# The second product of both MLPs as Strassen's seven products of halves

## The chip, the core and the metric

The kernel runs on one core of a Trainium2 chip. What counts is the time of one execution on the device in microseconds. The core's engines each work through a list of instructions of their own in a fixed order: PE (TensorE) multiplies matrices, PEld is its weight load, DVE (VectorE) and ACT (ScalarE) work element by element, POOL (GpSimd) does some sums, and SP issues the loads from memory. An instruction waits for another engine by a semaphore, and everything behind it in its engine's list waits with it. Sums of matmuls collect in PSUM, everything else lies in SBUF.

## The reference

Two transformer blocks run one after the other on 512 tokens of 1024 features (one batch), in fp32. Each ends with an MLP of 4096 hidden units; their lines are, cut to them:

```python
D_MODEL = 1024
SEQ = 512
D_FF = 4 * D_MODEL
...
        u = rmsnorm_2(x, norm_mlp_g[i]) @ w_up[i]
        x = x + jnp.square(jax.nn.relu(u)) @ w_down[i]
```

The first block's MLP has the same form, with `norm_ffn`, `ffn_w1` and `ffn_w2`. Its block holds a hybrid mixer (spatial gating and a gated delta rule) and a cross attention ahead of the MLP, and a last norm behind it. The second block has an mLSTM and a sliding-window attention ahead of its MLP, and behind it a gate with a small product of `p` (the PLE part).

## The kernel before, in words

All activations lie feature by feature: `x_fm` is x as 8 tiles of 128 features by 512 tokens, and a tile of a product is 128 features by 512 tokens in one PSUM bank. An fp32 product is made of three matmuls (`mm3`, L217 to L222): each operand is split into a high part rounded to the type fp32r and the low rest; high times high (L220), high times low (L221) and low times high (L222) are summed in the bank.

Weights come in pieces of 512 KB, 512 rows by 256 columns, through `wload` (L194 to L205): SP loads the piece into `wr` (2 buffers), ACT casts it to the high part `wh` (L203, 128x1024), DVE subtracts to get `wl` (L204); `wh` and `wl` have 3 buffers each. Two such pieces are a granule: the weights of two output tiles over a depth of 1024, 48 matmuls of 128x512 (`proj_fm` with `wgran`). All of it lies in one tile pool, `wp`, that is open for the whole program, so the loads, casts and subtractions of one stage's first granules stand ready while the stage before still multiplies.

The MLP (`ffn`) goes by quarters of 1024 hidden units. `up(q)` makes 8 hidden tiles in 4 granules: DVE does relu and the token's norm factor from PSUM (L804), ACT squares (L805), and `split_sb` (L261 on ACT, L262 on DVE) writes the high and the low part. `down(q)` is 4 granules of two output tiles each, and DVE adds each finished tile to `x_fm` (`add_res`, L401). H has two sets of buffers (slots 0 to 3 and 4 to 7), so the order is up 0, up 1, down 0, up 2, down 1, up 3, down 2, down 3: every down has another quarter's up ahead of it.

In the last down of an MLP the evacuation also makes the next norm's operands for the tile that has just been finished. Behind the first MLP (`between`) that is the scaled split (L264 on ACT, L265 on DVE) and two squares (L274 on ACT) that are summed into two accumulators (L276, on POOL, for the last tile on DVE); then `fin` sums over features on PE (L284, and a second such sum at L852). Behind the second MLP (`tail`) it is the split and one square.

The order in each engine's list is set by the framework's scheduler when the program is built, from the order in which the kernel writes the instructions and from which buffers come free; there is no order written by hand.

## Time and profile before

| | |
|---|---|
| median of 3 runs | 1758.17 us (1754.64 to 1764.05) |
| the profiled execution | 1758.89 us, its span 1757.1 us |
| mean granted TensorE clock | 0.992 |
| first MLP, roughly | 457 to 815 us of the span |
| second MLP, roughly | 1333 to 1695 us |
| loaded by the hardware queue | 153.64 MB, 27.4% of the DMA engines' time |

The span is the time from the first to the last instruction in the trace. A row of a timeline has the start and the duration in microseconds, engine, line, operation, what is written from what is read, the tile and, in brackets, how long the engine had been idle before it and who ended that. Matmuls overlap: what one costs is the distance from its start to the next one's. A row of a group has the count, the sum and the mean in ns. The windows view has, for each stretch, the busy time and the number of instructions of each engine, then the granted clock, the share of the DMA engines and GB/s.

### The profile page before, as it was taken

The page shows a single profiled execution, that of the slowest core. Times are in us where ns is not written, and L with a number is a line of the kernel's source. Part 1 is how long each engine was busy: PE and PEld are TensorE (multiplying, and loading weights), DVE is VectorE, ACT ScalarE, POOL GpSimd, SP SyncE. Part 2 cuts the span into 40 slices and gives each one's busy share as a digit, 9 for nine tenths or more (in the row PEclk, how much of TensorE's full clock was granted, in tenths as well). Part 3 has the DMA queues.
Part 4 walks back from the last instruction along what each step waited for, and adds up shares of the span by engine and source line. Part 5 has one row for each costly group of instructions (what it writes and reads, how often), then busy time and mean ns, then how long its engine had stood idle before and what let it go on. Part 6 is the DMA issues. An engine that isn't in the chain of part 4 may idle for free.

```text
span 1757.1 us, 22629 instructions
## 1 busy us (share of the span) xinstructions
PE 1719.7 (98%) x8740; PEld 1427.2 (81%) x8740; DVE 1011.4 (58%) x2039; ACT 720.9 (41%) x1254; POOL 148.4 (8%) x126
## 2 busy tenths in 40 slices
PE   7999999999999999999999999999999999999997
PEld 6987788877888888888888887788888888888886
DVE  6898886655543444446755469865555434344446
ACT  5344444444333333334444448654234323232343
POOL 2211321201000000012000000000120000000112
PEclk9999998999999999999999999999999999999999
DMA  5221232312222223223222321223222222323231
GB/s 196 88 72 61 71 97 77 118 51 72 96 97 96 93 89 95 95 86 95 73 73 74 95 73 49 72 73 96 86 97 89 91 95 96 96 96 108 90 102 61
DMA packets 49436, 155.09 MB, mean 88 GB/s; under 512 B 9392, under 2 KB 11696, under 8 KB 49328
## 3 DMA queue, kind: packets, MB, share of 16 engines
q1 hardware_dynamic: 49328, 153.64, 27.4%
q8 instruction: 69, 1.13, 0.3%
q14 instruction: 39, 0.32, 0.1%
HBM read 151.26 MB, written 2.10 MB: 87 GB/s over the span
## 4 chain that ended last, share of the span: by engine, by line
PE 87%; DVE 9%; ACT 2%; issue 2%; DMA 0%; POOL 0%; SPq 0%; DVEq 0%; ACTq 0%
PE psd L221 26%; PE psd L222 26%; PE psd L220 26%; DVE wl L204 1%; PE c L563 1%; ACT wh L203 1%; PE lg L1147 1%; PE po L1174 1%; PE c L512 1%; PE m L1068 1%; DVE S L368 1%; DVE e L319 1%; PE pss L1169 0%; PE m L1076 0%; DVE dA L583 0%
## 5 line engine op out<-in xcount | busy, mean ns | idle before, releaser
L220 PE MATMUL psd<-S,wh 128*128 128x512 f32 (+1 forms) x1968 | 770.5, 392 | 6.3 <-ACT wh L203 6.3
L222 PE MATMUL psd<-S,wl 128*128 128x512 f32 (+1 forms) x1968 | 774.3, 394 | 1.3 <-DVE wl L204 1.3
L221 PE MATMUL psd<-S,wh 128*128 128x512 f32 (+1 forms) x1904 | 748.1, 393 | 2.4 <-DVE S L265 2.3
L204 DVE TENSOR_TENSOR wl<-wr,wh 128x1024 fp32r<-128x1024 f32 (+3 forms) x281 | 349.4, 1243 | 227.0 <-ACT wh L203 225.9
L203 ACT CAST wh<-wr 128x1024 fp32r<-128x1024 f32 (+3 forms) x281 | 292.0, 1039 | 434.3 <-PE psd L221 406.5
L220 PEld LDWEIGHTS psd<-S,wh 128*128 128x128 f32 x1968 | 372.7, 189 | 86.2 <-ACT wh L203 7.2
L222 PEld LDWEIGHTS psd<-S,wl 128*128 128x128 f32 x1968 | 371.5, 189 | 79.8 <-DVE wl L204 2.3
L221 PEld LDWEIGHTS psd<-S,wh 128*128 128x128 f32 x1904 | 358.7, 188 | 80.6 <-DVE S L265 4.2
L276 POOL TENSOR_TENSOR acc<-acc,sq 128x512 f32<-128x512 f32 (+1 forms) x47 | 67.9, 1446 | 916.8 <-ACT sq L274 916.3
L401 DVE TENSOR_TENSOR x_fm<-psd,x_fm 128x512 f32<-128x512 f32 x88 | 60.7, 690 | 137.8 <-PE psd L222 137.7
L221 PE MATMUL psd<-wl,S 128*128 128x256 f32 (+2 forms) x480 | 137.4, 286 | 0.6 <-DVE wl L204 0.6
L222 PE MATMUL psd<-wh,S 128*128 128x256 f32 (+2 forms) x480 | 137.1, 286 | 0.0
L220 PE MATMUL psd<-wh,S 128*128 128x256 f32 (+2 forms) x480 | 136.5, 284 | 0.0
L804 DVE SCALAR_TENSOR_TENSOR e<-psd,bc 128x512 f32<-128x512 f32 x64 | 44.3, 691 | 112.2 <-PE psd L222 109.3
L805 ACT ACTIVATE e<-e 128x512 f32<-128x512 f32 x64 | 40.4, 632 | 135.1 <-DVE e L804 135.1
L221 PEld LDWEIGHTS psd<-wl,S 128*128 128x128 f32 x480 | 91.6, 191 | 1.4 <-DVE wl L204 1.0
L220 PEld LDWEIGHTS psd<-wh,S 128*128 128x128 f32 x480 | 91.8, 191 | 0.4
L222 PEld LDWEIGHTS psd<-wh,S 128*128 128x128 f32 x480 | 91.8, 191 | 0.1
L262 DVE TENSOR_TENSOR S<-e,S 128x512 fp32r<-128x512 f32 (+1 forms) x84 | 56.7, 675 | 49.2 <-ACT S L261 49.2
L261 ACT CAST S<-e 128x512 fp32r<-128x512 f32 (+1 forms) x84 | 50.5, 601 | 42.9 <-POOL e L931 27.1
L264 ACT ACTIVATE S<-x_fm,vec 128x512 fp32r<-128x512 f32 x40 | 28.9, 721 | 55.4 <-DVE x_fm L401 36.9
L319 DVE SCALAR_TENSOR_TENSOR e<-e,vec,e 128x511 f32<-128x511 f32 (+2 forms) x60 | 46.6, 779 | 2.6 <-ACT e L316 2.2
(411 smaller groups left out, 1459.7 us busy)
## 6 DMA issues: line engine op xcount, KB each, us to landing
wr<-in_ffn_w_dram SPq DMA_DIRECT2D x64, 512.0 KB
wr<-in_w_up_dram SPq DMA_DIRECT2D x32, 512.0 KB
wr<-in_w_down_dram SPq DMA_DIRECT2D x32, 512.0 KB
wr<-in_w_in_qk_dram SPq DMA_DIRECT2D x16, 512.0 KB
wr<-in_w_in_v_dram SPq DMA_DIRECT2D x12, 512.0 KB
wr<-in_xa_wk_dram SPq DMA_DIRECT2D x8, 512.0 KB
wr<-in_xa_wv_dram SPq DMA_DIRECT2D x8, 512.0 KB
wr<-in_xa_wq_dram SPq DMA_DIRECT2D x8, 512.0 KB
```

The costliest lines, as they stand in the source:

```text
L203: nc.scalar.copy(hi[:, c], raw[:, c])
L204: nc.vector.tensor_tensor(out=lo[:, c], in0=raw[:, c], in1=hi[:, c].bitcast(F32), op=ALU.subtract)
L220: mm(ps, ah, bh, start=first, stop=False)
L221: mm(ps, ah, bl, start=False, stop=False)
L222: mm(ps, al, bh, start=False, stop=last)
L261: nc.scalar.copy(hi, src)
L262: nc.vector.tensor_tensor(out=lo, in0=src, in1=hi.bitcast(F32), op=ALU.subtract)
L276: eng.tensor_tensor(out=acc, in0=acc, in1=sq, op=ALU.add)
L319: nc.vector.scalar_tensor_tensor(out=c[:, s:], in0=xr[:, :T - s], scalar=w(j), in1=c[:, s:], op0=ALU.mult, op1=ALU.add)
L401: self.nc.vector.tensor_tensor(out=self.x[:, o], in0=ps, in1=self.x[:, o], op=ALU.add)
L804: nc.vector.scalar_tensor_tensor(out=t, in0=ps, scalar=0.0, in1=bc, op0=ALU.max, op1=ALU.mult)
L805: nc.scalar.activation(t, t, AF.Square)
```

## The change

The second product of both MLPs is computed with Strassen's scheme in Winograd's form. For each pair of output tiles the product over 1024 hidden units is taken as a 2x2 block product: two output tiles by the two halves of the hidden units on the one side, the two halves of the hidden units by two halves of the tokens (256 each) on the other. Seven block products take the place of eight. Each is 4 hidden tiles deep, so 4 x 3 matmuls of 128x256, 84 a granule in place of 48 of 128x512.

- The hidden operand: `st_fill` makes four sums and differences of 128x256 on DVE for each pair of hidden tiles, and splits seven blocks (7 x 256 columns in place of 2 x 512) into high and low parts.
- The weights: `st_weights` loads three pieces on SP (512, 512 and 256 KB); a DMA issued by POOL adds the fourth quarter to both halves of the second piece (512 KB, `accum_op`), which gives two of the four weight sums; two DVE additions of 128x512 give the others. Seven blocks are split, in pieces of 1024, 1024, 1024 and 512 columns.
- The products: `st_gemm` puts them into three banks. X takes products 0, 3, 5 and 6, each added to the bank's content; Z takes 2 and 4; Y takes 1. After each product DVE adds or subtracts the bank in one 256-token half of an output tile of x: 7 instructions of 128x256 in place of 2 of 128x512. A later product of the same bank therefore waits for DVE's earlier reading.
- The order: up and down follow each other quarter by quarter, with one set of H. The norm work of the last quarter (`post`) follows the granule.
- The pools: `wp` is closed and opened anew around each MLP, with 5 buffers in place of 3 for `wh` and `wl` there, beside a pool `fp` and a PSUM pool `px`. Slots are renamed to fit, xattn's output pairs and the PLE part's tiles lie elsewhere, and `p` is loaded at the start of `tail`.
- The weights of the second product are laid out by `halves` before the launch.

```diff
+    @contextmanager
+    def weights(self, bufs=3):
+        with self.tc.tile_pool(name=self.uid("wp"), bufs=bufs) as self.wp:
+            yield
...
-        mm(ps, ah, bh, start=first, stop=False)
-        mm(ps, ah, bl, start=False, stop=False)
-        mm(ps, al, bh, start=False, stop=last)
+        mm(ps, ah, bh, start=first, stop=False, skip_group_check=more)
+        mm(ps, ah, bl, start=False, stop=False, skip_group_check=more)
+        mm(ps, al, bh, start=False, stop=last, skip_group_check=more)
...
-        up(0)
-        up(1)
-        down(0, self.add_res)
-        up(2)
-        down(1, self.add_res)
-        up(3)
-        down(2, self.add_res)
-        down(3, evac)
...
+    def st_fill(self, H, k, e1, e2):
+        nc = self.nc
+        TT, STT = nc.vector.tensor_tensor, nc.vector.scalar_tensor_tensor
+        t = H[0]
+        h = (slice(0, 256), slice(256, 512))
+        ms = self.t(self.fp, [P, 4, 256], "ms", bufs=1)
+        TT(out=ms[:, 3], in0=e2[:, h[1]], in1=e1[:, h[1]], op=ALU.subtract)
+        TT(out=ms[:, 1], in0=e1[:, h[0]], in1=e1[:, h[1]], op=ALU.subtract)
+        STT(out=ms[:, 2], in0=ms[:, 3], scalar=-1.0, in1=e1[:, h[0]], op0=ALU.mult, op1=ALU.subtract)
+        STT(out=ms[:, 0], in0=ms[:, 2], scalar=-1.0, in1=e2[:, h[0]], op0=ALU.mult, op1=ALU.subtract)
+        self.split_sb(t[6][:, 0, k], t[6][:, 1, k], e1[:, h[0]])
+        self.split_sb(t[4][:, :, k], t[5][:, :, k], e2.rearrange("p (a c) -> p a c", a=2))
+        self.split_sb(t[2][:, :, k], t[3][:, :, k], ms[:, 2:4])
+        self.split_sb(t[0][:, :, k], t[1][:, :, k], ms[:, 0:2])
+    def st_weights(self, src):
+        nc = self.nc
+        r0 = self.t(self.wp, [P, 2, T], "wr", bufs=2)
+        r1 = self.t(self.wp, [P, 1, T], "wr1", bufs=2)
+        ss = self.t(self.wp, [P, 2, T], "ws", bufs=2)
+        nc.sync.dma_start(r0, src[:, 0:2])
+        nc.sync.dma_start(ss, src[:, 0:3:2])
+        nc.sync.dma_start(r1, src[:, 2:3])
+        nc.gpsimd.dma_start(ss, src[:, 3:4].broadcast_to([P, 2, T]), accum_op=ALU.add)
+        out = []
+        def split(raw):
+            n = raw.shape[1]
+            hi, lo = self.t(self.wp, [P, n, T], "wh", F32R), self.t(self.wp, [P, n, T], "wl", F32R)
+            self.split_sb(hi, lo, raw)
+            out.extend((hi[:, i], lo[:, i]) for i in range(n))
+        split(r0)
+        split(ss)
+        s2 = self.t(self.wp, [P, 2, T], "ws2", bufs=1)
+        nc.vector.tensor_tensor(out=s2[:, 0], in0=ss[:, 0], in1=r1[:, 0], op=ALU.add)
+        nc.vector.tensor_tensor(out=s2[:, 1], in0=s2[:, 0], in1=r0[:, 1], op=ALU.add)
+        split(s2)
+        split(r1)
+        a11, a12, s3, s1, s2, s4, a22 = out
+        return a11, a12, s1, s2, s4, s3, a22
+    def st_gemm(self, src, H, o1, post):
+        nc = self.nc
+        TT = nc.vector.tensor_tensor
+        w = self.st_weights(src)
+        _, hi, lo = H
+        X, Z = (self.t(self.px, [P, T], "x")[:, :256] for _ in range(2))
+        Y = self.psd()[:, :256]
+        x = [[self.x[:, o1 + n, t * 256:t * 256 + 256] for t in range(2)] for n in range(2)]
+        def prod(i, ps, m, first):
+            ah, al = w[i]
+            for k in range(4):
+                c = slice(k * P, (k + 1) * P)
+                self.mm3(ps, ah[:, c], al[:, c], hi[m][:, k], lo[m][:, k], first and k == 0, k == 3, not first)
+        def add(n, t, ps, op=ALU.add):
+            TT(out=x[n][t], in0=x[n][t], in1=ps, op=op)
+        prod(0, X, 0, True)
+        add(0, 0, X)
+        prod(1, Y, 1, True)
+        add(0, 0, Y)
+        prod(2, Z, 4, True)
+        add(1, 1, Z, ALU.subtract)
+        prod(3, X, 5, False)
+        add(0, 1, X)
+        prod(4, Z, 2, False)
+        add(0, 1, Z)
+        prod(5, X, 6, False)
+        add(1, 1, X, ALU.subtract)
+        prod(6, X, 3, False)
+        add(1, 0, X, ALU.subtract)
+        for o in (o1, o1 + 1):
+            post(o)
+    def ffn(self, w1, w2, xh, xl, acc, slots, post):
+        nc = self.nc
+        with self.tc.tile_pool(name=self.uid("px"), bufs=4, space=PSUM) as self.px:
+            rs = self.tok_rs(acc, "rs")
+            bc = self.tok_bc(rs, "bc")
+            for q in range(4):
+                H = None
+                for g in range(4):
+                    es = []
+                    def ev(o, ps):
+                        e = self.t(self.fp, [P, T], "eh", bufs=4)
+                        nc.vector.scalar_tensor_tensor(out=e, in0=ps, scalar=0.0, in1=bc, op0=ALU.max, op1=ALU.mult)
+                        nc.scalar.activation(e, e, AF.Square)
+                        es.append(e)
+                    self.proj_fm(self.wgran(w1, 4 * q + g), xh, xl, (2 * g, 2 * g + 1), ev)
+                    H = H or self.st_operand(slots)
+                    self.st_fill(H, g, *es)
+                for g in range(4):
+                    self.st_gemm(self.D[w2][4 * q + g], H, 2 * g, post if q == 3 else lambda o: None)
...
-        K.setup()
-        K.mixer()
-        mem = K.memory()
-        with tc.tile_pool(name="sp2", bufs=1) as K.sp2:
-            op = K.w_out1()
-            op = K.xattn(*op, mem)
+        with K.weights():
+            K.setup()
+            K.mixer()
+            mem = K.memory()
+            with tc.tile_pool(name="sp2", bufs=1) as K.sp2:
+                op = K.w_out1()
+                op = K.xattn(*op, mem)
+        with K.weights(5), tc.tile_pool(name="fp", bufs=1) as K.fp:
+            K.sp2 = K.fp
             ev, fin = K.between()
-            K.ffn("ffn_w1", "ffn_w2", *op, ev)
+            K.ffn("ffn_w1", "ffn_w2", *op, (0, 1, 4, 7, 8, 9, 10), ev)
             op2 = fin()
-        mh, ml = K.mixer2(*op2)
-        with tc.tile_pool(name="sp3", bufs=1) as K.sp2:
-            xh, xl = K.pair((9, 10)), K.pair((11, 12))
+        with K.weights():
+            K.perm = [2, 3, 5, 6, 0, 1, 4, 7, 8]
+            mh, ml = K.mixer2(*op2)
+            K.perm = list(range(13))
+            xh, xl = K.pair((0, 1)), K.pair((4, 7))
...
+        with K.weights(5), tc.tile_pool(name="fp", bufs=1) as K.fp:
+            K.sp2 = K.fp
             ev, ple = K.tail()
-            K.ffn("w_up_2", "w_down_2", xh, xl, acc, ev)
+            K.ffn("w_up_2", "w_down_2", xh, xl, acc, (2, 3, 5, 6, 8, 9, 10), ev)
...
+def halves(w):
+    v = w.reshape(4, 2, P, -1, 2, P).transpose(3, 2, 4, 1, 0, 5).reshape(-1, P, 4, 4 * P)
+    return v[:, :, [0, 1, 3, 2]]
...
```

The order of the lists outside the two MLPs stays as it was. Three places show what has moved. The names: `wr`, `wr1` and `ws` are raw weights, `ws2` the two sums made by DVE, `wh` and `wl` their high and low parts, `S` a slot (parts of H or of the next operand), `e1` and `eh` the hidden tile, `x` and `psd` PSUM banks, `x_fm` the residual.

DVE in the middle of the first down, before: additions of finished tiles and subtractions for the weights' low halves take turns.

```order
L401 TENSOR_TENSOR x_fm_73<-psd_910_5128,x_fm_73 128x512
L204 TENSOR_TENSOR wl_917_5188<-wr_915_5186,wh_916_5187 128x1024
L401 TENSOR_TENSOR x_fm_73<-psd_911_5154,x_fm_73 128x512
L204 TENSOR_TENSOR wl_922_5246<-wr_920_5244,wh_921_5245 128x1024
L401 TENSOR_TENSOR x_fm_73<-psd_918_5192,x_fm_73 128x512
L204 TENSOR_TENSOR wl_925_5252<-wr_923_5250,wh_924_5251 128x1024
```

The same place after:

```order
L846 TENSOR_TENSOR ws2_902_5124<-ws_897_5111,wr1_896_5110 128x512
L870 TENSOR_TENSOR x_fm_73<-x_fm_73,psd_894_5017 128x256
L269 TENSOR_TENSOR wl_899_5117<-wr_895_5109,wh_898_5116 128x1024
L870 TENSOR_TENSOR x_fm_73<-x_fm_73,x_893_5016 128x256
L269 TENSOR_TENSOR wl_901_5121<-ws_897_5111,wh_900_5120 128x1024
L870 TENSOR_TENSOR x_fm_73<-x_fm_73,x_892_5015 128x256
L847 TENSOR_TENSOR ws2_902_5124<-ws2_902_5124,wr_895_5109 128x512
L870 TENSOR_TENSOR x_fm_73<-x_fm_73,x_893_5016 128x256
L269 TENSOR_TENSOR wl_904_5128<-ws2_902_5124,wh_903_5127 128x1024
L870 TENSOR_TENSOR x_fm_73<-x_fm_73,x_892_5015 128x256
L269 TENSOR_TENSOR wl_906_5132<-wr1_896_5110,wh_905_5131 128x512
L870 TENSOR_TENSOR x_fm_73<-x_fm_73,x_907_5135 128x256
```

Between the subtractions (L269) now stand seven additions into x (L870) and the two weight sums (L846, L847) of each granule; each L870 waits for a product, and what stands behind it waits with it.

ACT at the end of an up, before the first down. The rows before: the last hidden tile's square (L805) and cast stand behind a weight cast for the next granule.

```order
L203 CAST wh_908_5123<-wr_907_5122 128x1024
L203 CAST wh_913_5181<-wr_912_5180 128x1024
L805 ACTIVATE e1_903_5111<-e1_903_5111 128x512
L261 CAST S5_861_4825<-e1_903_5111 128x512
L203 CAST wh_916_5187<-wr_915_5186 128x1024
L203 CAST wh_921_5245<-wr_920_5244 128x1024
L203 CAST wh_924_5251<-wr_923_5250 128x1024
```

And after, where the down that follows reads this very tile:

```order
L903 ACTIVATE eh_861_4825<-eh_861_4825 128x512
L268 CAST S10_830_4612<-eh_861_4825 128x256
L268 CAST wh_875_4891<-wr1_866_4870 128x512
L268 CAST wh_883_4996<-wr_880_4989 128x1024
L903 ACTIVATE eh_863_4853<-eh_863_4853 128x512
L268 CAST S8_828_4610<-eh_863_4853 128x2x256
L268 CAST wh_885_5000<-ws_882_4991 128x1024
L268 CAST S4_826_4608<-ms_864_4856 128x2x256
```

The cast of `wh_883`, for the second granule of the down, stands ahead of the last hidden tile's square (L903); the operand's casts S8, S4 and S0 follow, with another weight cast between them.

ACT at the end of the first MLP, before: the weight casts of the next stage (`wh_1162`, `wh_1165`) stand among the last tiles' work.

```order
L203 CAST wh_1162_6868<-wr_1161_6867 128x1024
L264 ACTIVATE S1_804_4498<-x_fm_73,g12_802_4495 128x512
L274 ACTIVATE sq_1121_6699<-x_fm_73 128x512
L274 ACTIVATE sq_1122_6702<-x_fm_73,vec_74 128x512
L264 ACTIVATE S1_804_4498<-x_fm_73,g12_802_4495 128x512
L274 ACTIVATE sq_1130_6745<-x_fm_73 128x512
L274 ACTIVATE sq_1131_6748<-x_fm_73,vec_74 128x512
L203 CAST wh_1165_6874<-wr_1164_6873 128x1024
```

And after:

```order
L281 ACTIVATE sq_1274_7834<-x_fm_73 128x512
L281 ACTIVATE sq_1275_7837<-x_fm_73,vec_74 128x512
L271 ACTIVATE S3_1214_7423<-x_fm_73,g12_804_4503 128x512
L281 ACTIVATE sq_1276_7842<-x_fm_73 128x512
L281 ACTIVATE sq_1277_7845<-x_fm_73,vec_74 128x512
L210 CAST wh_1306_7936<-wr_1305_7935 128x1024
L210 CAST wh_1309_7942<-wr_1308_7941 128x1024
```

The first cast for the next stage's weights (`wh_1306`) has moved behind the whole work on the last output tiles.

72 lines of the change are left out of this document (30 added, 42 removed).

## The prediction

> **What bounds the kernel now.** I read the page's busy shares and its chain of waits first, then the busy time of each engine in the stretches of the two MLPs.
>
> ```profile
> span 1757.1 us, 22629 instructions
> PE 1719.7 (98%) x8740; PEld 1427.2 (81%) x8740; DVE 1011.4 (58%) x2039; ACT 720.9 (41%) x1254; POOL 148.4 (8%) x126
> PE 87%; DVE 9%; ACT 2%; issue 2%; DMA 0%; POOL 0%; SPq 0%; DVEq 0%; ACTq 0%
> ...
> core 0: us, PE busy (x) PEld busy (x) DVE busy (x) ACT busy (x) POOL busy (x), PEclk, DMA share, GB/s
> 460.00:815.00 355.00, 355.00 (x1533) 287.22 (x1533) 153.42 (x170) 120.86 (x153) 17.06 (x14) 1.00 0.29 94
> 1333.00:1695.00 362.00, 362.00 (x1562) 292.93 (x1561) 153.15 (x174) 122.12 (x157) 8.80 (x6) 1.00 0.29 95
> ```
>
> PE is busy 98% of the span and is 87% of the chain. In both MLPs (the two stretches) it is busy in every microsecond at clock 1.00, while DVE works 43% and the DMA engines 29%. So two things hold there: fewer matmul microseconds come off the end one for one, and every new wait of PE comes back one for one. Nothing that is idle now can be sped up; only PE's own time can be bought, and the price is paid wherever PE is made to wait.
>
> **Term 1, the matmuls.** A granule of the second product is 48 matmuls of 128x512 now and 7x4x3 = 84 of 128x256 after. What one costs is its distance to the next, not its own duration, since they overlap.
>
> ```profile
> 800.10 0.39 PE L222 MATMUL psd<-S,wl 128*128 128x512 f32 x1
> ...
> 805.66 0.39 PE L222 MATMUL psd<-S,wl 128*128 128x512 f32 x1
> ...
> 1729.89 0.28 PE L220 MATMUL psd<-S,wh 128*128 128x256 f32 x1
> ...
> 1735.46 0.28 PE L222 MATMUL psd<-S,wl 128*128 128x256 f32 x1
> ```
>
> The first pair lies 24 matmuls apart: 5.56/24 = 0.2317 us each. The second pair is the first and the last of a run of 48 in the PLE gate: 5.57/47 = 0.1185 us. A granule goes from 48 x 0.2317 = 11.12 to 84 x 0.1185 = 9.95 us, 1.17 less, and over 32 granules **-37 us**. The 48 are enough to see that a new weight load for every 256 columns does not slow them, so I keep this term narrow (-35 to -39).
>
> **Term 2, three seams.** The weight pool is now closed and opened again around each MLP, with other tiles laid over it. A new pool's first load or first cast therefore has to wait until the old pool's last matmul has read its weights; before, the next granules' weights lay ready. PE has nothing else then. The prices:
>
> ```profile
> 1691.51 3.06 SPq L200 DMA_DIRECT2D wr<-in_w_ple_gate_dram  x2
> 1695.22 1.05 ACT L203 CAST wh<-wr 128x1024 fp32r<-128x1024 f32 x1 [1.09 <-DMA wr<-in_w_ple_gate_dram]
> ...
> 565.30 0.39 PE L222 MATMUL psd<-S,wl 128*128 128x512 f32 x1
> 565.73 0.69 DVE L401 TENSOR_TENSOR x_fm<-psd,x_fm 128x512 f32<-128x512 f32 x1 [0.74 <-PE psd L222]
> ...
> L264 ACT ACTIVATE S<-x_fm,g 128x512 fp32r<-128x512 f32 x8 | 5.8, 726 | 16.4 <-DVE x_fm L401 16.4
> L274 ACT ACTIVATE sq<-x_fm 128x512 f32<-128x512 f32 x47 | 29.0, 618 | 5.9 <-DVE x_fm L1220 5.8
> ...
> 455.95 0.96 PE L284 MATMUL pss<-ones,acc 128*128 128x1 f32 x8
> 456.78 0.47 PE L221 MATMUL psd<-S,wh 128*128 128x512 f32 x1
> ...
> L204 DVE TENSOR_TENSOR wl<-wr,wh 128x1024 fp32r<-128x1024 f32 x269 | 337.2, 1254 | 225.1 <-ACT wh L203 224.0
> ```
>
> A 512 KB load takes 3.71 us from issue to the cast that waited for it (1691.51 to 1695.22), the cast 1.05. After a tile's last matmul (start 565.30, slot 0.23) the engine that waits starts 0.2 us later (565.73). The third matmul on a new weight needs the low half, 1.25 behind the cast, with two matmuls (0.46) before it: 0.8 more. PE has the sums for the norm to do in any case, 0.83 (455.95 to 456.78). Seam into MLP 1: 0.2 + 3.71 + 1.05 + 0.05 to restart PE + 0.8 = 5.8, less 0.83: 5.0. Seam behind MLP 1: the load is early, but its cast stands on ACT behind the last tile's scaled copy and two squares: 0.2 + 0.45 (add of 256 columns, below) + 0.73 + 2 x 0.62 + 1.05 = 3.7, its low half behind the small norm operations on DVE, some 1.5 more, less two such sums (1.66): 3.6. Seam into MLP 2, with an evacuation of 0.69 and one square: 0.2 + 0.69 + 0.73 + 0.62 + 1.05 + 0.05 + 0.8 = 4.1, less 0.83: 3.3. Behind MLP 2 the small product with p stands between, so 0. Together **+12** (9 if the casts come a step earlier, 15 if nothing of PE's lies inside).
>
> **Term 3, the clock after such a gap.**
>
> ```profile
> 274.36 0.38 PE L563 MATMUL c<-dTb,dT 128*128 128x32 f32 x2 [2.30 <-DVE doy L169]
> ...
> 275.30:284.80 9.50, 9.50 (x45) 9.50 (x46) 4.48 (x13) 2.98 (x5) 0.00 (x0) 0.50 0.25 88
> ...
> 19.50:22.50 3.00, 3.00 (x9) 2.20 (x8) 3.00 (x5) 1.26 (x2) 0.00 (x0) 0.57 0.69 269
> ...
> 18.09 0.50 PE L221 MATMUL psd<-S,wh 128*128 128x512 f32 x1 [2.03 <-DVE S L265]
> ```
>
> A wait of 2.30 us was followed by 9.5 us at a granted clock of 0.50 with PE always busy; a wait of 2.03 by some 3 us at 0.57. Half clock costs half its length, 1.3 to 4.8 us. Three seams of 3.3 to 5 us: **+8** (4 to 14). The Trainium skill, "TensorE: Matmul & The Clock Gate", in the first part on the gate's two states, puts the fall to half clock behind at least one idle window of about 3.4 us. By that rule the shortest seam would stay at full clock and the sum would be 2 to 3 lower, an estimate; the rows above, gaps of 2.30 and 2.03 us, speak against it.
>
> **Term 4, from up to down, eight times.** Until now down(q-1) lay behind up(q), so its operand had been ready for one quarter. Now down(q) follows up(q) at once. Product 0 needs only the first hidden tile of the last pair, product 1 the other. On ACT that tile's square stands behind a cast whose buffer is freed by the last up matmul. The durations and what DVE takes back to back:
>
> ```profile
> L804 DVE SCALAR_TENSOR_TENSOR e<-psd,bc 128x512 f32<-128x512 f32 x64 | 44.3, 691 | 112.2 <-PE psd L222 109.3 <-ACT bc L298 2.9
> L805 ACT ACTIVATE e<-e 128x512 f32<-128x512 f32 x64 | 40.4, 632 | 135.1 <-DVE e L804 135.1
> L261 ACT CAST S<-e 128x512 fp32r<-128x512 f32 x76 | 47.2, 621 | 35.3 <-POOL e L931 27.1 <-DVE e L394 6.2
> L262 DVE TENSOR_TENSOR S<-e,S 128x512 fp32r<-128x512 f32 x76 | 53.4, 703 | 49.0 <-ACT S L261 49.0
> ...
> 811.08 0.68 DVE L401 TENSOR_TENSOR x_fm<-psd,x_fm 128x512 f32<-128x512 f32 x1
> 811.84 1.26 DVE L204 TENSOR_TENSOR wl<-wr,wh 128x1056 fp32r<-128x1056 f32 x1
> 813.01 0.74 DVE L265 SCALAR_TENSOR_TENSOR S<-x_fm,g,S 128x512 fp32r<-128x512 f32 x1
> 813.68 0.68 DVE L276 TENSOR_TENSOR acc<-acc,sq 128x512 f32<-128x512 f32 x1
> 814.28 0.68 DVE L276 TENSOR_TENSOR S<-S,sq 128x512 f32<-128x512 f32 x1
> ```
>
> From the end of the last up matmul: the cast is done after 0.2 + 1.05 = 1.25 (the relu beside it after 0.9), the square after 1.9, the operand's cast after 2.5, its low half after 3.2. PE has product 0 (12 x 0.1185 = 1.42) and three quarters of product 1 (1.07): 2.5. It waits 0.7, up to 1.0 where the low half finds DVE occupied. Eight times: **+6.5** (0 if the cast's buffer comes free earlier, 13 if two of st_fill's additions of some 0.4 stand ahead of the low half as well).
>
> **Term 5, inside down.** DVE does now, per granule, two additions of 512 from PSUM (0.76 each, from 811.08 to 811.84) and two subtractions of 1024 (1.17, to 813.01): 3.9 of 11.1 us. After: seven additions of 256 columns, two sums of 512 (0.60, from 813.68 to 814.28), subtractions of 3 x 1024 + 512. A 256-column instruction from PSUM isn't in the trace in this form; from below half of 0.76 is 0.38, with rows in SBUF around it:
>
> ```profile
> L1163 DVE TENSOR_SCALAR lg<-lg,sm 128x256 f32<-128x256 f32 x48 | 14.1, 349 | 0.3
> L1084 DVE SCALAR_TENSOR_TENSOR S<-S,hh 128x256 f32<-128x256 f32 x16 | 6.8, 423 | 4.1 <-ACT hh L1069 3.8
> ```
>
> I take 0.42 (0.35 to 0.50): 7 x 0.42 + 2 x 0.60 + 3 x 1.17 + 0.6 = 8.25 of the 9.95 us. DVE stays under PE's time, but its order is fixed, and PE now depends on it inside a granule. One bank X takes products 0, 3, 5 and 6: product 6 may not go on accumulating until DVE has read product 5 out, and between the two PE has one product of 1.42 us (the next granule's first). If a subtraction of 1024 has just begun, DVE is back after up to 1.17, and reads for 0.42: 0.2 + 1.17 + 0.42 = 1.8, 0.4 late; the same shape stands between products 2 and 4 and between 3 and 5. I followed DVE's order by hand through a granule with these durations: 0.25 to 0.55 us of waiting per granule, 0.28 taken: **+9** for 32 (0 if the subtractions happen to fall beside the long products, 18 at 0.55).
>
> **Term 6, the last quarters.** Four granules of each MLP now have the norm's work for two tiles behind the seven additions, and POOL's sums slow DVE:
>
> ```profile
> 797.90 2.10 DVE L204 TENSOR_TENSOR wl<-wr,wh 128x1024 fp32r<-128x1024 f32 x1 [1.39 <-ACT wh L203]
> 800.69 1.23 DVE L204 TENSOR_TENSOR wl<-wr,wh 128x1024 fp32r<-128x1024 f32 x1
> ```
>
> Beside POOL's sums of squares the subtraction takes 2.10 instead of 1.23. With 2 x 0.75 and up to 2 x 0.87 DVE has 8.25 + 1.5 + 1.7 = 11.5 us for 9.95: 1.5 late in each of 4 granules of MLP 1, half of it in MLP 2, where one sum in place of two is taken; part of it is term 5 already. **+5** (2 to 12).
>
> **Term 7, the accumulating DMA.** No transfer with an addition, and none issued by POOL, is in the trace. From below it costs nothing: a down granule has 1.25 MB of plain loads (3.71 us for 0.5 MB alone; the engines are 29% busy now) and two buffers of each, so about 20 us of allowance. From above: if it takes over some 14 us from issue to landing, every granule waits. Nearest row: the plain load, 3.71, so **0**. The Trainium skill, "Collectives: The Full Stack", in the part on the bandwidth ceiling (why a reduce-scatter is half of an all-gather), says that an addition in a DMA reads two sources and so runs at half the rate. By it the 0.5 MB would cost the engines some 2 x 1.6 = 3.2 us in 9.95, an estimate that still leaves them time; no row of this trace shows such a transfer.
>
> **Sum.** -37 + 12 + 8 + 6.5 + 9 + 5 + 0 = +3.5 us. The profiled execution took 1758.89 with a span of 1757.1, and lies 0.7 over the median of the runs (1758.17), so it may stand for them: 1758.9 + 3.5 = **1762 us**.
>
> **The rivals.** (1) *The products run clean.* The seams stay, but the scheduler's order lets the additions fall between the subtractions, term 4 is half, term 5 is 2, term 6 is 2, term 3 is 4: -37 + 12 + 4 + 3 + 2 + 2 = -14, **1745**. For it: 8.25 of 9.95 leaves DVE free time, and my walk through its order is only as good as the durations in it. Against it: the dependence through bank X is new and its distance is one product. (2) *DVE's fixed order binds in down.* If a 256-column addition takes 0.55 or more (its fixed part is large: 0.349 already for a one-input instruction from SBUF), DVE needs 9.2 us plus its waits for PE's products, and each granule is 0.9 late in place of 0.28: +20, **1782**. It decides from the point where DVE's work and its waits pass 9.95 us. For it: the order is static and additions stand between subtractions; against it: half the 512 row is 0.38. (3) *The accumulating transfer is late.* From about 14 us on its landing sets the pace; 1.2 us more per granule gives +38, **1800**. For it: it starts only when the plain load before it has landed, and POOL issues it in its own order, behind the sums of squares of the last quarters; against it: 20 us of allowance. That the change does not do what it says is excluded by the order, in which the 84 narrower matmuls of each granule stand.
>
> **How the numbers follow.** A measurement of this kernel can tell about 0.5% from no change, here 8.8 us: faster is under 1749.4, slower over 1767.0. The forecast (own range 1750 to 1774): 0.47, of it 0.03 faster, 0.33 same, 0.11 slower. Rival 1: 0.27, of it 0.25 faster, 0.02 same. Rival 2: 0.17, of it 0.01 same, 0.16 slower. Rival 3: 0.09, all slower. Faster 0.28, same 0.36, slower 0.36. The range takes rival 1 down to where terms 2 and 3 are at their low ends too (3 + 4 less: 1738) and rival 2 up to where term 6 is at its double (1786); left out are rival 3 and the far end of rival 1.
>
> **What would show it.** Term 1: 128x256 products in down at a pitch near 0.1185; 0.125 would take 17 us off the gain. Term 2: three waits of PE of 3.3 to 5 us, the longest before the first up granule, ended by the cast. Term 3: slices with a clock of 0.5 behind them. Term 4: eight waits below 1 us ended by the operand's low half. Term 5: waits of PE in down ended by DVE's additions into x, in sum 9 us, and DVE busy above 80% there. Term 7: waits of the weight casts ended by the accumulating transfer. The forecast is wrong if PE's waits inside the eight downs exceed 25 us in all, or stay under 5.

## The result and the profile after

The changed kernel takes 1785.43 us (median of 4 runs, 1780.85 to 1789.62) against 1761.11 us before in the same job, a ratio of 1.0151 with a 95% interval of 1.0125 to 1.0176. It is slower by 24 us where 3.5 were forecast. Its profiled execution took 1789.62 us with a span of 1787.9, 30.8 us more than the span before. From its page, the busy shares and the chain of waits by engine:

```profile
span 1787.9 us, 25673 instructions
PE 1718.1 (96%) x9892; PEld 1477.1 (83%) x9892; DVE 1226.2 (69%) x2519; ACT 800.2 (45%) x1382; POOL 188.5 (11%) x158
PE 75%; DVE 12%; DMA 5%; ACT 4%; issue 3%; POOL 0%; SPq 0%; DVEq 0%; ACTq 0%
```

PE is as busy as before (1718 against 1720 us) although its products have become cheaper; its mean granted clock is 0.980 in place of 0.992, and a matmul at half clock counts as busy. PE's share of the chain fell from 87% to 75%, and DMA, which had 0%, has 5%. The timeline of PE has what it waited for. The last bracket of a row is the idle time ahead of it and who ended that:

```profile
459.15 1.05 PE L291 MATMUL pss<-ones,acc 128*128 128x1 f32 x8 [2.92 <-DVE acc L283]
...
461.16 0.80 PE L227 MATMUL psd<-S,wh 128*128 128x512 f32 x1 [0.95 <-ACT wh L210]
...
512.71 0.39 PE L227 MATMUL psd<-S,wh 128*128 128x256 f32 x1 [0.66 <-ACT S L268]
553.06 0.39 PE L227 MATMUL x<-S,wh 128*128 128x256 f32 x1 [1.63 <-DVE x_fm L870]
...
609.52 0.28 PE L228 MATMUL x<-S,wh 128*128 128x256 f32 x1
...
618.65 0.28 PE L227 MATMUL psd<-S,wh 128*128 128x256 f32 x1
...
641.59 0.58 PE L227 MATMUL x<-S,wh 128*128 128x256 f32 x1 [2.38 <-DVE x_fm L870]
...
731.38 0.39 PE L227 MATMUL x<-S,wh 128*128 128x256 f32 x1 [2.24 <-DVE x_fm L870]
...
806.38 0.39 PE L227 MATMUL x<-S,wh 128*128 128x256 f32 x1 [2.17 <-DVE x_fm L870]
...
818.40 0.36 PE L227 MATMUL x<-S,wh 128*128 128x256 f32 x1 [2.82 <-DVE x_fm L870]
...
829.89 1.84 PE L291 MATMUL pss<-ones,acc 128*128 128x1 f32 x8 [2.75 <-DVE acc L283]
...
1352.74 1.05 PE L291 MATMUL pss<-ones,acc 128*128 128x1 f32 x8 [2.93 <-DVE acc L283]
...
1370.49 0.50 PE L229 MATMUL psd<-S,wl 128*128 128x512 f32 x1 [1.78 <-DVE wl L211]
```

459.15, 829.89 and 1352.74 are the three seams. Each has two waits: first for DVE's last sum of squares, since no product on ready weights covers it any more, and behind the norm's sums for the new weights (461.16 with 0.95; 0.74 and 0.98 us at the other two, part of it for the norm's small operations). Together they are about 11.3 us, near the 12 of term 2, but of the longer waits none is ended by the cast. 512.71 is the only wait of that kind at a change from up to down. 553.06, 641.59 and 731.38 are something that the prediction had no term for: the change from a down to the next up. There the scheduler has put the last product of a down's last granule behind the first 6 matmuls of the next up, and it waits for DVE's addition of the product before it. 806.38 and 818.40 lie in the first MLP's last down, and 1370.49 in the first up of the second MLP; it is read below. Between 609.52 and 618.65 stand 77 matmuls without a gap: 0.1186 us each.

What stands ahead of that addition at 553.06, from the timeline of all engines:

```profile
542.09 1.19 POOL L834 DMA_DIRECT2D ws<-in_ffn_w_dram  x1 [8.30 <-DVE x_fm L870]
...
545.08 7.94 SPq L207 DMA_DIRECT2D wr<-in_ffn_w_dram  x3
...
550.36 1.05 ACT L210 CAST wh<-wr 128x1024 fp32r<-128x1024 f32 x1 [5.17 <-DMA wr<-in_ffn_w_dram]
551.45 1.23 DVE L211 TENSOR_TENSOR wl<-wr,wh 128x1024 fp32r<-128x1024 f32 x1 [2.38 <-ACT wh L210]
...
552.59 0.42 DVE L870 TENSOR_TENSOR x_fm<-x_fm,x 128x256 f32<-128x256 f32 x1
```

Read from below: the addition (552.59) stands behind the subtraction for the next up's weights (551.45); that waited 2.38 us for ACT's cast, and the cast 5.17 us for the load, the first of the three issued from 545.08 on. From issue to cast it took 5.3 us; the plain load of the prediction took 3.71. The adding transfer, issued at 542.09, was under way beside it until 548.97. At the six such changes the load took 4.2 to 6.2 us to its cast, and PE waited 0.58 to 2.59 us there, each time some 3.65 us less than its load took. DVE had nothing else to do and PE needed only the addition. A late load stops PE although the data of the load are not yet wanted.

In the first up of the second MLP DVE itself waits for the adding transfer:

```profile
1368.01 0.69 DVE L846 TENSOR_TENSOR ws<-ws,wr 128x512 f32<-128x512 f32 x1 [9.31 <-DMA ws<-in_w_down_dram]
```

This is the first weight sum for the coming down; DVE idled 9.31 us ahead of it. Behind it in DVE's list stands the subtraction for the up's weights that PE waits for at 1370.49: 1.78 us, 3.8 with the half clock that followed. In the first MLP DVE idles 8.49 us ahead of the same sum (473.67), and PE does not wait.

The last down of the first MLP, DVE and POOL beside each other:

```profile
799.35 7.44 POOL L283 TENSOR_TENSOR acc<-acc,sq 128x512 f32<-128x512 f32 x4 [4.07 <-ACT sq L281]
...
802.01 1.98 DVE L269 TENSOR_TENSOR wl<-wr,wh 128x1024 fp32r<-128x1024 f32 x1
...
803.91 1.75 DVE L272 SCALAR_TENSOR_TENSOR S<-x_fm,g,S 128x512 fp32r<-128x512 f32 x1
805.59 0.41 DVE L870 TENSOR_TENSOR x_fm<-x_fm,psd 128x256 f32<-128x256 f32 x1
805.92 0.41 DVE L870 TENSOR_TENSOR x_fm<-x_fm,x 128x256 f32<-128x256 f32 x1
```

While POOL sums squares, DVE's subtraction takes 1.98 and its scaled split 1.75 us (0.75 alone), and the addition for which PE waits at 806.38, that of bank X at 805.92, comes after them. The windows of four places around or behind waits:

```profile
460.00:465.00 5.00, 4.05 (x11) 2.90 (x12) 4.41 (x15) 2.10 (x2) 0.95 (x1) 0.54 1.00 326
815.00:820.00 5.00, 2.18 (x14) 2.01 (x14) 4.00 (x5) 0.00 (x0) 2.37 (x2) 0.88 0.00 0
830.00:835.00 5.00, 4.74 (x19) 4.47 (x20) 1.61 (x11) 2.09 (x2) 0.00 (x0) 0.50 0.33 129
1370.00:1375.00 5.00, 4.51 (x13) 3.62 (x14) 2.93 (x5) 2.20 (x4) 0.00 (x0) 0.68 0.57 150
```

The column behind the busy times is the granted clock: 0.54 and 0.50 behind the first two seams; behind the third it was 0.50 from 1354.74 to 1358.15. The other two windows are no seams: 0.88 around the wait at 818.40, and 0.68 behind the wait at 1370.49.

### The profile page after: what moved, and what is told of

Its sections match the earlier page's. It is cut to its first block, busy times and chain, and to the rows that moved or that the text cites. A ratio compares the mean times of both kernels' runs of the same rounds, so it can differ in the third digit from the quotient of the medians.

```text
span 1787.9 us, 25673 instructions
## 1 busy us (share of the span) xinstructions
PE 1718.1 (96%) x9892; PEld 1477.1 (83%) x9892; DVE 1226.2 (69%) x2519; ACT 800.2 (45%) x1382; POOL 188.5 (11%) x158
## 3 DMA queue, kind: packets, MB, share of 16 engines
q1 hardware_dynamic: 58032, 162.03, 28.6%
q0 software_dynamic: 8704, 16.78, 5.8%
## 4 chain that ended last, share of the span: by engine, by line
PE 75%; DVE 12%; DMA 5%; ACT 4%; issue 3%; POOL 0%; SPq 0%; DVEq 0%; ACTq 0%
PE psd L228 18%; PE psd L229 18%; PE psd L227 18%; PE x L227 4%; PE x L228 4%; PE x L229 4%; DVE wl L211 2%; DMA wr<-in_ffn_w_dram 2%; ACT wh L210 2%; DVE wl L269 1%; PE c L570 1%; DVE S L272 1%; DMA wr<-in_w_up_dram 1%; DVE x_fm L870 1%; PE lg L1231 1%
## 5 line engine op out<-in xcount | busy, mean ns | idle before, releaser
L227 PE MATMUL psd<-S,wh 128*128 128x512 f32 (+1 forms) x1584 | 614.4, 388 | 9.2 <-ACT wh L210 7.5
L229 PE MATMUL psd<-S,wl 128*128 128x512 f32 (+1 forms) x1584 | 610.6, 386 | 3.1 <-DVE wl L211 3.1
L228 PE MATMUL psd<-S,wh 128*128 128x512 f32 (+1 forms) x1520 | 587.6, 387 | 2.1 <-DVE S L272 2.1
L211 DVE TENSOR_TENSOR wl<-wr,wh 128x1024 fp32r<-128x1024 f32 (+4 forms) x217 | 268.9, 1239 | 153.0 <-ACT wh L210 152.5
L227 PEld LDWEIGHTS psd<-S,wh 128*128 128x128 f32 x1584 | 303.6, 192 | 68.0 <-ACT wh L210 8.5
L228 PEld LDWEIGHTS psd<-S,wh 128*128 128x128 f32 x1520 | 290.8, 191 | 58.5 <-DVE S L272 3.0
L210 ACT CAST wh<-wr 128x1024 fp32r<-128x1024 f32 (+4 forms) x217 | 224.5, 1036 | 231.8 <-PE psd L228 111.1
L227 PE MATMUL x<-S,wh 128*128 128x256 f32 x768 | 219.4, 292 | 19.9 <-DVE x_fm L870 18.8
L228 PE MATMUL x<-S,wh 128*128 128x256 f32 x768 | 216.0, 283 | 0.0
L229 PE MATMUL x<-S,wl 128*128 128x256 f32 x768 | 215.2, 283 | 0.0
L227 PEld LDWEIGHTS x<-S,wh 128*128 128x128 f32 x768 | 144.6, 191 | 28.5 <-DVE x_fm L870 20.1
L228 PEld LDWEIGHTS x<-S,wh 128*128 128x128 f32 x768 | 146.8, 191 | 0.4
L229 PEld LDWEIGHTS x<-S,wl 128*128 128x128 f32 x768 | 146.3, 191 | 0.0
L870 DVE TENSOR_TENSOR x_fm<-x_fm,x 128x256 f32<-128x256 f32 x192 | 78.7, 417 | 50.0 <-PE x L229 48.8
L269 DVE TENSOR_TENSOR wl<-ws,wh 128x1024 fp32r<-128x1024 f32 x64 | 81.3, 1271 | 20.6 <-ACT wh L268 20.5
```

The source lines that it names most:

```text
L210: nc.scalar.copy(hi[:, c], raw[:, c])
L211: nc.vector.tensor_tensor(out=lo[:, c], in0=raw[:, c], in1=hi[:, c].bitcast(F32), op=ALU.subtract)
L227: mm(ps, ah, bh, start=first, stop=False, skip_group_check=more)
L228: mm(ps, ah, bl, start=False, stop=False, skip_group_check=more)
L229: mm(ps, al, bh, start=False, stop=last, skip_group_check=more)
L269: nc.vector.tensor_tensor(out=lo, in0=src, in1=hi.bitcast(F32), op=ALU.subtract)
```

## The experiments

All ratios are to the kernel before, run in the same job, where it took 1755 to 1761 us. "Less than the changed kernel" is a difference of medians from different jobs and good to some 2 us. "Down" is the time from a down's first 256-column matmul to the next 512-column one.

**1 to 4: one suspect each.** The first was meant to free a buffer early for the late load; the second takes POOL's sums away; the third the adding transfer; the fourth the seams.

```diff
-nc.vector.tensor_tensor(out=s2[:, 1], in0=s2[:, 0], in1=r0[:, 1], op=ALU.add)
+nc.vector.tensor_tensor(out=s2[:, 1], in0=s2[:, 0], in1=r1[:, 0], op=ALU.add)
```

> The fourth weight sum adds the third piece (r1) once more in place of the first piece (r0), so the output is not the reference's; the number of instructions is the same, but r0's buffer comes free after its low half instead of after DVE's second sum. Theory (late load): the wait of PE at the start of each up (1.5 to 2.6 us, seven times, with half clock behind some) comes from the first weight load of that up, which waits for r0's buffer; with it free earlier the waits shrink below 0.5 us and the time falls by 10 to 15 us, to about 1773. Rival (order): the addition of product 5 stands behind a subtraction of the up's weights in DVE's list whatever the load does; the waits stay and the time stays within 4 us of 1785.

Measured: 1790.82 us, ratio 1.0193 (1.0157 to 1.0228). The waits at the changes from down to up are 1.2 to 2.9 us, no shorter than before. At the first of them the load is issued 4.78 us ahead of the change in both kernels, so it was not this buffer that it waited for; the theory fell.

```diff
             eng = nc.gpsimd if k < KT - 1 else nc.vector
-            eng.tensor_tensor(out=acc, in0=acc, in1=sq, op=ALU.add)
+            if not skip or k == KT - 1:
+                eng.tensor_tensor(out=acc, in0=acc, in1=sq, op=ALU.add)
```

> Leaves out the sums of squares of the first MLP's last quarter for the tiles 1 to 6 (12 additions on POOL), so the next norm is wrong; everything else stays. Theory (POOL beside DVE): the last down of the first MLP takes 53.6 us in place of 39.8 because POOL's sums make DVE's instructions beside them 0.4 to 1.1 us longer; without them it takes 42 to 45 and the time falls by 9 to 12 us, to about 1775. Rival (number of instructions): DVE's own list is too long and its order too stiff there; the last down stays above 50 us and the time within 4 us of 1785.

Measured: 1775.28 us, 1.0093 (1.0066 to 1.0120), 10 us less than the changed kernel. The last down with the seam's wait behind it fell from 53.6 to 45.3 us, and DVE's rows there, from the timeline, are as long as anywhere else:

```profile
785.55 0.74 DVE L272 SCALAR_TENSOR_TENSOR S<-x_fm,g,S 128x512 fp32r<-128x512 f32 x1
...
786.88 1.21 DVE L269 TENSOR_TENSOR wl<-ws,wh 128x1024 fp32r<-128x1024 f32 x1
```

So it is POOL's company that costs there, not the number of DVE's instructions.

```diff
-        nc.gpsimd.dma_start(ss, src[:, 3:4].broadcast_to([P, 2, T]), accum_op=ALU.add)
```

> Leaves out the accumulating transfer on POOL (32 of 512 KB); the two sums are then just the loaded pieces, and the output is not the reference's. Theory (hidden): no wait of PE ends with that transfer, its landing lies ahead of its use, and the time stays within 4 us of 1785. Rival (late transfer): DVE's weight sums wait for it (18 us in all), and what stands behind them on DVE waits with them; the time falls by 6 us or more.

Measured: 1767.76 us, 1.0047 (1.0022 to 1.0073), 17.7 us less. The expected "hidden" is wrong. Of the waits at the six changes from down to up one is left, 0.16 us (553.36 in its timeline), and the wait at 1370.49 is gone; the downs (39.6 us) did not change. The load at the first change, in its timeline:

```profile
546.86 1.79 SPq L207 DMA_DIRECT2D wr<-in_ffn_w_dram  x2
...
550.67 1.05 ACT L210 CAST wh<-wr 128x1024 fp32r<-128x1024 f32 x1 [3.70 <-DMA wr<-in_ffn_w_dram]
```

From issue to cast it is 3.8 us in place of 5.3, and 3.5 to 3.8 at all six. The transfer costs at the change to the next up, not inside the down that it serves.

```diff
-        with K.weights(5), tc.tile_pool(name="fp", bufs=1) as K.fp:
+        with tc.tile_pool(name="fp", bufs=1) as K.fp:
...
-            hi, lo = self.t(self.wp, [P, n, T], "wh", F32R), self.t(self.wp, [P, n, T], "wl", F32R)
+            if own:
+                hi, lo = self.t(self.fp, [P, n, T], "wh2", F32R, bufs=2), self.t(self.fp, [P, n, T], "wl2", F32R, bufs=2)
+            else:
+                hi, lo = self.t(self.wp, [P, n, T], "wh", F32R), self.t(self.wp, [P, n, T], "wl", F32R)
```

> Computes the same. One weight pool with 3 buffers stays open for the whole program; only the pieces that Strassen needs besides lie in the MLP's own pool, with 2 buffers for the split sums. Theory (seams): the three seams, where PE waits for the first weights behind a closed pool, with the half clock behind them, cost 20 to 24 us of the 1785; with the weights ahead the time falls by 14 to 20 us, to about 1768. Rival (buffers): what the seams give is lost to the 3 + 2 buffers in place of 5, and the time falls by less than 6 us.

Measured: 1764.87 us, 1.0038 (1.0017 to 1.0059), 20.6 us less. The three seam waits are gone: PE has no idle time around any of the three sums for a norm. In this frame the changes from down to up have no wait either, but the downs take 41.3 to 44.4 us instead of 39.7.

**5 and 6: the transfer's kind, and the frame alone.**

```diff
-        nc.gpsimd.dma_start(ss, src[:, 3:4].broadcast_to([P, 2, T]), accum_op=ALU.add)
+        nc.gpsimd.dma_start(ss, src[:, 3:4].broadcast_to([P, 2, T]))
```

> POOL still issues the 32 transfers, of the same 512 KB from the same source, but they overwrite instead of adding, so the output is not the reference's. Theory (the addition): an adding transfer holds the DMA engines about twice as long as a plain one of its size (5.8% of the span for 16.78 MB against 28.6% for 162 MB), and the first weights of the next up come late behind it; overwriting gives back half or more of what leaving the transfers out gave (17.7 us), so 1772 to 1777. Rival (one more transfer in the way, whatever its kind): the time stays within 4 us of 1785.

Measured: 1774.75 us, 1.0096 (1.0070 to 1.0122), 10.7 us less. The queue table of the changed kernel and then of this one, with packets, MB and the share of 16 engines' span:

```profile
q1 hardware_dynamic: 58032, 162.03, 28.6%
q0 software_dynamic: 8704, 16.78, 5.8%
```

```profile
q0 software_dynamic: 4608, 16.78, 3.7%
...
ws<-in_ffn_w_dram POOLq DMA_DIRECT2D x16, 512.0 KB, 5.3
ws<-in_w_down_dram POOLq DMA_DIRECT2D x16, 512.0 KB, 4.8
```

Per MB the adding transfer holds the engines 5.8/16.78 against 28.6/162.03, 1.96 times a plain load on SP's queue. Against the same transfer without the addition it is 5.8/3.7, 1.57 times, and only this isolates the addition. The rule of the Trainium skill that was weighed ahead ("Collectives: The Full Stack", the part on the bandwidth ceiling: an addition reads two sources, half the rate) agrees with the first number and is above the second. 5.8% of 1787.9 us over 32 transfers is 3.24 us of the engines for each, 2.05 without the addition. Its median landing is 6.3 and 6.1 us after issue, 5.3 and 4.8 without the addition. About 11 of its 18 us are the addition, the other 7 that it is one more transfer.

```diff
-                    self.st_gemm(self.D[w2][4 * q + g], H, 2 * g, post if q == 3 else lambda o: None)
+                    self.proj_fm(self.wgran(w2 + "p", 4 * q + g), hh, hl, (2 * g, 2 * g + 1), evd)
```

> Computes the same. The change's frame (pools closed and opened around each MLP, up and down of a quarter one after the other, one set of H, norm work behind the tile) with the plain second product of before. Theory (the frame costs): seams with their half clock take about 8 us each, and each up to down switch something; the time is 1778 to 1790, so what Strassen saves (37 us) and what its additions and transfers cost inside the frame about cancel. Rival (Strassen's own work costs): the frame alone is within 8 us of before, 1755 to 1769.

Measured: 1782.19 us, 1.0139 (1.0102 to 1.0176): the frame without any Strassen is 23 us slower than before, and the changed kernel 2 to 3 us slower than that, which the two intervals do not tell apart. In its timeline PE waits at the seams alone:

```profile
455.56 1.42 PE L291 MATMUL pss<-ones,acc 128*128 128x1 f32 x8 [2.93 <-DVE acc L283]
457.45 0.79 PE L227 MATMUL psd<-S,wh 128*128 128x512 f32 x1 [0.48 <-ACT wh L210]
...
822.12 1.84 PE L291 MATMUL pss<-ones,acc 128*128 128x1 f32 x8 [3.02 <-DVE acc L283]
...
1344.68 1.05 PE L291 MATMUL pss<-ones,acc 128*128 128x1 f32 x8 [2.93 <-DVE acc L283]
```

**7 to 12: is there a form that is faster?** All with one pool. Finer subtractions, then the plain product in the first MLP's last quarter:

```diff
-            self.split_sb(hi, lo, raw)
+            nc.scalar.copy(hi, raw)
+            for i in range(n):
+                nc.vector.tensor_tensor(out=lo[:, i], in0=raw[:, i], in1=hi[:, i].bitcast(F32), op=ALU.subtract)
```

> Computes the same. As the kernel with one pool, but DVE's subtractions for the low halves in down are made in pieces of 512 columns in place of 1024. Theory (fixed order on DVE): PE's waits of 0.5 to 1.3 us in down end with additions into x that stand behind subtractions of 1.17 us; with pieces of 0.6 the waits about halve, and the downs, 41.4 to 46.6 us plus a last product, fall by 1 to 2 us each: 1752 to 1759 against 1765. Rival (DVE has too much to do): the pieces cost as much as they save; within 4 us of 1765.

> Computes the same. As the kernel with one pool and the finer subtractions, and the last quarter of the first MLP by the plain product. Theory (DVE beside POOL's sums): Strassen in that quarter saves 4.7 us of matmuls but its last down is 6 to 8 us over its matmuls; plain gives 2 to 4 us: 1749 to 1757. Rival: with the finer pieces the last down is clean already, and plain costs 2 to 5 us.

Measured: 1764.23 us, 1.0025 (1.0010 to 1.0041): the finer pieces change nothing. 1757.18 us, 0.9993 (0.9971 to 1.0016) with the plain quarter: no difference from before, 7 us from the one quarter. In the downs, DVE's first weight sum now waits for the adding transfer; the waits view of the latter has 29 us of that:

```profile
DVE ws L851 <- DMA ws<-in_w_down_dram: 14.7, 6, 7.0
DVE ws L851 <- DMA ws<-in_ffn_w_dram: 14.1, 5, 6.9
```

So a third buffer was tried, with the sums in place to make room:

```diff
-ss = self.t(self.fp, [P, 2, T], "ws", bufs=2)
+ss = self.t(self.fp, [P, 2, T], "ws", bufs=3)
...
-        s2 = self.t(self.fp, [P, 2, T], "ws2", bufs=1)
+        s2 = ss
```

> Computes the same. As the kernel with one pool, finer subtractions and the plain last quarter in the first MLP, with 3 buffers in place of 2 for the piece into which the transfer adds, DVE's two sums made in place (no buffer of their own) and 2 buffers for the hidden tiles. Theory (adding transfer too late): DVE's first weight sum waits about 2 us for the adding transfer in a granule, and the additions into x behind it make PE wait 0.7 to 1.2; with one more buffer the transfer starts a granule earlier and the downs fall from 41-42.6 to about 39.7: 1748 to 1753. Rival (DVE's work): its waits only move to other places in the order; within 3 us of 1757.

> Computes the same. As the kernel before, but Strassen in all quarters of both MLPs. Theory (POOL's sums beside a full DVE list): 4 to 8 us slower than with the plain last quarter of the first MLP, 1753 to 1761. Rival: with the earlier transfer DVE has room there too; 0 to 4 us faster, since one more quarter is saved.

> Computes the same. As the first kernel of this set, with the subtractions in down in pieces of 1024. Theory (fixed order on DVE): 2 to 6 us slower than with pieces of 512. Rival (size of the pieces does not matter): within 2 us of it.

> Computes the same. One pool, up and down quarter by quarter, and the plain product in all quarters: the frame without seams and without Strassen. Theory (the seams are all that the frame costs): within 4 us of before, 1755 to 1763. Rival (the order up, down costs too): 6 us or more above before.

Measured: 1774.51 us, 1.0095 (1.0063 to 1.0127) with the third buffer, 1791.70 us, 1.0193 (1.0169 to 1.0218) with Strassen in all quarters, 1777.67 us, 1.0117 (1.0090 to 1.0144) with coarse pieces. The downs but for the last lost their waits as expected, but the changes from down to up had waits again, up to 3.64 us in the first and 4.49 in the second, and the theory (1748 to 1753 us for the first) missed by 20. Early transfers for the next down now stood ahead of the up's loads. The plain product everywhere in this frame gave 1759.32 us, 1.0013 (0.9990 to 1.0035): the order up, down costs nothing that can be measured (the interval allows up to 6 us), and the frame's 23 us are the seams.

**13 and 14: the order of the loads.**

```diff
+        if tok is not None:
+            nc.gpsimd.tensor_copy(out=ss[:, 0, 0:1], in_=tok)
+            nc.gpsimd.tensor_copy(out=r1[:, 0, 0:1], in_=tok)
         nc.sync.dma_start(r0, src[:, 0:2])
```

> Computes the same. In the changed kernel, the second and third piece of the next down's first two granules get two one-column copies by POOL ahead of their loads, which wait for a hidden tile of the up's second granule; so these loads and the adding transfer, which are not needed for 45 us, no longer stand ahead of the next up's first loads. Theory (order of loads): the waits of PE at the six changes from down to up (0.7 to 2.8 us and their half clock, 14 to 15 us in all) nearly vanish, as without the adding transfers: 1768 to 1774. Rival (the transfers of the running down fill the DMA engines): the first loads are as late as before, within 4 us of 1785.

> Computes the same. The kernel with one pool, finer subtractions, 3 buffers for the sums and the plain last quarter in the first MLP, with the same holding back. Theory (order of loads): its downs were free of waits but the changes from down to up took 3 to 4.5 us each, five times; with the loads held back 15 to 20 us go: 1752 to 1760, not slower than before. Rival: 1770 and more.

Measured: 1782.75 us, 1.0151 (1.0113 to 1.0190), and 1796.26 us, 1.0218 (1.0191 to 1.0245). In the first the six waits at the changes from down to up did go (the 6 matmuls there take 1.56 to 1.66 us, 1.39 at their pitch), as the theory of the order has it; the time did not. The downs rose from 39.7 to 41.0 to 42.1 us (40.4 for the first), with a wait for ACT at their second product that was not there before, as in its timeline:

```profile
595.81 0.39 PE L227 MATMUL psd<-S,wh 128*128 128x256 f32 x1 [1.12 <-ACT S L268]
```

In the second, the last granule of an up waited 3.7 to 4.7 us for its weights' casts. Why the first was no faster stands in its trace: DVE's first weight sum now waits 2.6 to 6.3 us in each of the eight ups and starts less than 0.1 us after the landing of the held-back transfer. The longest of the first MLP:

```profile
754.14 0.69 DVE L849 TENSOR_TENSOR ws<-ws,wr 128x512 f32<-128x512 f32 x1 [5.68 <-DMA ws<-in_ffn_w_dram]
```

What stands behind it in DVE's list is late with it: the relu of the up's second-last tile starts 4.8 us after its product (590.81), 0.6 in the changed kernel, and so the down's operand is late. The order decides where the transfer's lateness is paid; moving it did not make it cheaper.

**15 and 16: all four sums by DVE.**

```diff
-nc.sync.dma_start(r1, src[:, 2:3])
-nc.gpsimd.dma_start(ss, src[:, 3:4].broadcast_to([P, 2, T]), accum_op=ALU.add)
+nc.sync.dma_start(r1, src[:, 2:4])
+nc.vector.tensor_tensor(out=ss[:, 0], in0=ss[:, 0], in1=r1[:, 1], op=ALU.add)
+nc.vector.tensor_tensor(out=ss[:, 1], in0=ss[:, 1], in1=r1[:, 1], op=ALU.add)
```

> Computes the same. In the changed kernel all four weight sums are DVE's: the third and the fourth piece come in one plain load, two more additions of 512 columns a granule replace the adding transfer, and the hidden tiles have 2 buffers in place of 4. DVE then has about 9.4 of 9.95 us a granule. Theory (the adding transfer costs through DVE's list): the waits at the changes from down to up go as without the transfers (15 to 18 us), and the extra 1.2 us on DVE gives back 5 to 12 in the downs: 1772 to 1780. Rival (DVE full): each granule gets 0.5 us or more, 16 in all, so 1783 or more.

> Computes the same. The same sums in the kernel with one pool, finer subtractions and the plain last quarter in the first MLP (1757). Theory: its downs wait for the adding transfer (41 to 42.6 us in place of 39.8); without it they fall to 40 to 41: 1746 to 1755, below before. Rival (DVE full): 1758 or more.

Measured: 1766.50 us, 1.0053 (1.0029 to 1.0076), 17 to 19 us less than the changed kernel, although DVE has two more additions in every granule; its downs are 39.4 to 39.5 us. The rival of a full DVE fell. In the frame with one pool: **1738.08 us, 0.9887 (0.9846 to 0.9929)**, 17 us faster than before. Its page:

```profile
span 1737.2 us, 25369 instructions
PE 1698.5 (98%) x9748; PEld 1456.7 (84%) x9748; DVE 1234.9 (71%) x2599; ACT 792.1 (46%) x1366; POOL 148.5 (9%) x126
...
PE 85%; DVE 10%; ACT 2%; issue 2%; DMA 0%; POOL 0%; SPq 0%; DVEq 0%; ACTq 0%
```

DMA has left the chain and PE has 85% of it. The six downs that are not the last of an MLP take 39.3 to 39.4 us, and behind them no wait is left.

## Why the prediction was wrong

The terms, as forecast and as the profile of the changed kernel has them:

| term | forecast | measured, and from what |
|---|---|---|
| 1 the matmuls | -37 | -37: 0.1186 us in 77 intervals |
| 2 and 3 seams and clock | +20 | about +22 in the profile (7.7, 8.4 and 5.8 around the three seams); +23 as the frame alone |
| 4 up to down | +6.5 | about +4: an idle wait of 0.66 at the first down, which has 40.5 us in place of 39.7, and in each down some 0.45 at the first products, for the operand's last cast and low half |
| 5 inside down | +9 | about +7: 324 of the 336 matmuls take 39.67 us, 38.42 at their pitch; 1.25 in each of 8 downs, less the 0.45 of term 4 |
| 6 last quarters | +5 | +12: the last downs have 50.9 and 43.7 us of 39.9, less the 1.25 above each |
| 7 adding transfer | 0 | about +19: 15 at the six changes from down to up (12 of waits, 3 of half clock) and 4 in the first up of the second MLP; +17.7 by leaving it out |
| sum | +3.5 | about +27 of the profile's 30.8; 4 are not placed |

**The step that failed** is term 7, "Nearest row: the plain load, 3.71, so 0". It asked whether the transfer lands before its own sums are needed, with "about 20 us of allowance", and that held inside the downs: nothing there waited for it, but for the first sums of each MLP, which DVE takes in the first up. What it missed is who comes behind it. The DMA engines deliver the next up's first weights late (4.2 to 6.2 us from issue to cast, 3.5 to 3.8 without the transfer), DVE's subtraction of them stands in a fixed order ahead of an addition that PE needs, and so the lateness of a load that has time reaches PE through DVE's list. The first sums of the second MLP reach PE in the same way, at 1370.49. So a term of 0 was about 18 us: leaving the transfers out gave 17.7, replacing them by additions 17 to 19. The estimate of 3.2 us of the engines for each transfer was right (3.24 measured); "still leaves them time" was the wrong question, for the engines' share in a down rose from 0.29 to 0.60 (597.98 to 637.65), and a load that comes beside them takes longer. The rival on the transfer had the right culprit and the wrong place: 1.2 us in every granule, "from about 14 us on"; it lands in 6.3 and charges at six quarters' ends and once in an up.

**Terms that were mis-sized.** Term 6 had the mechanism (POOL's sums beside DVE), with 1.5 us a granule in the first MLP; it was about 2.4 (9.7 over 4 granules), since the scaled split suffers too (1.75 for 0.75) and the stretches were taken for the subtractions alone. Taking 12 of POOL's additions away gave 10 us. Terms 2 and 3 were 2 to 3 us small: behind MLP 1 the first weights' load was not early, as the prediction put it, but issued at 827.21, behind the last product, and ACT waited for it. Term 4 was some 2 us too large; why, no run shows.

**What held.** The pitch of the narrow matmuls, the waits inside down (9 against 7), three seams with half clock behind each, and that the frame and the gain would about cancel: the frame alone is at 1782, the change at 1785. The rival in which DVE's order binds in down forecast 1782, near the result, by another way: DVE's additions take 0.42 us as taken, DVE is 78% busy in a down, its waits there are about 7 us and not 29, and two further additions of 0.6 a granule did not slow the kernel. The measured 1785.43 lies just inside the upper end of the stated range, 1786, but that end was this rival with term 6 doubled; that the time came out there by term 7 is luck.

The changed kernel could have been faster by its own idea. With the seams closed, DVE's sums in place of the adding transfer, and the plain product where POOL works beside DVE, 28 of the 32 granules save 33 us by term 1 and 17 arrive. These three gave it together with the finer subtractions, which changed nothing by themselves; what each is worth inside that last kernel was not tried.

## What to carry to other kernels

A transfer that is on time for its own reader can still be late for the next reader of the DMA engines: price it by the first load that is queued behind it, and look in the engines' fixed order for what stands behind that load. Where PE is busy all the time, every pool that is closed and opened between stages is a stall of 3 us and more plus the half clock behind it (23 us for three seams here); keep the weight pool open and put only the extra tiles in a scope. When a version with a good idea is slower, run its frame without the idea first: here the frame alone cost 23 us, and the idea's gain of 37 was used up by costs of its own, of which the adding transfer was the largest.
